# Router queries on fp32 weights as they are, and one first-layer slot in eight multiplied on GpSimd

## Chip, cores and metric

The kernel runs on one core of one Trainium2 chip. The metric is the device time of one execution in microseconds (us), the median of several runs. Beside it one execution was recorded by the hardware profiler; every duration below is from that execution.

## What is computed

An encoder block for 256 tokens (and 16 meta tokens) of width 2048: gated linear attention and differential attention from one input projection, an output projection, and then a retrieval layer (PEER) over 16384 single-neuron experts. The change lies in the last one. Per token and head (8 heads) it makes a query, scores it against two sets of 128 sub-keys, takes the best 16 of each, the best 16 of the 256 sums, and reads those 16 experts' rows `u` and `v` of 2048 numbers:

```python
qb = (xb @ w_q).reshape(TB, PEER_HEADS, 2, PEER_DKEY)
s = jnp.einsum('thpc,hpnc->thpn', qb, sub_keys).astype(jnp.float32)
sv, si = lax.top_k(s, K)
...
cv, ci = lax.top_k(cand, K)
eidx = jnp.take_along_axis(cidx, ci, axis=-1)
g = jax.nn.softmax(cv, axis=-1)
u = u_tab[eidx]
vv = v_tab[eidx]
a = jax.nn.gelu(jnp.einsum('thkd,td->thk', u, xb).astype(jnp.float32), approximate=False)
return jnp.einsum('thk,thkd->td', (g * a).astype(vv.dtype), vv)
```

The dot products of `u` with the token (`thkd,td->thk`) are the first expert layer. A token has 8 x 16 = 128 such **slots**.

## The kernel before

Tokens stand in two tiles of 128 (`tt` = 0, 1), one token per partition. Up to about 1150 us of the profiled execution the kernel does the two attention branches and the output projection. Products with weights go through `proj` (L190): the fp32 weights (`raw`) are split by `load_half` (L163) into a rounded half `hi` (ACT, L185) and a remainder `lo` (a subtraction, L186), and TensorE (PE) makes three products of them, L200 to L202, with the activations split likewise.

The router follows. `hg` (L667, L668) is the normalized input of the layer, transposed and split into two halves. `queries(h)` makes the queries of head `h` with `proj`, where `lo` is computed on DVE for head 0 and on POOL (GpSimd) for the others; then the sub-key scores (L790), and `route(0, h)` (L714), which takes the top 16 (`top16`, L708 to L712) on DVE, with two casts (L721, L732) and one product (L736) on POOL, and leaves the experts' numbers in `ent`. The weights of the queries are loaded by SP's queue.

`gather_dots(tt, h)` (L746) goes over the 16 slots of a head: an indirect DMA issued by POOL (L751) gathers for each of 128 tokens its expert's row of 8 KB, 1 MB in all, and one DVE instruction multiplies it with the tokens `xb` and sums over the 2048 columns (L754):

```python
nc.gpsimd.indirect_dma_start(out=g, out_offset=None, in_=u_tab,
                             in_offset=bass.IndirectOffsetOnAxis(ap=ei[:, k:k + 1], axis=0))
s = h * 16 + k
nc.vector.scalar_tensor_tensor(g, g, 1.0, xb[:, tt, :], op0=ALU.mult, op1=ALU.mult,
                               accum_out=dots[tt][:, s:s + 1])
```

There are 256 such gathers and dots. The gathered tiles alternate between two pools of three buffers, `g` and `gr`; `gr` shares its buffers with the weights `raw`. Between the heads of tile 0 stand the routes of tile 1, between those of tile 1 the steps of `build_w0` on ACT and PE (L815 to L821), which builds the table W0 of the weights of tile 0. Its first use on DVE is at L898. After the last dot (about 1975 us) come W1, the second expert layer, dense on PE for one part of the columns and gathered for the other, and the last norm.

A scheduler writes each engine's queue ahead of time, from the program and its own estimates of durations; on the chip every queue runs in order, and POOL's queue holds its arithmetic and the issue of the gathers alike.

Of the kernel before, what the change touches and what calls it, by code (L numbers as in the profile page):

```python
# [10 lines left out]
F32 = mybir.dt.float32  # L11
F32R = mybir.dt.float32r
# [3 lines left out]
AF = mybir.ActivationFunctionType  # L16
ALU = mybir.AluOpType
# [3 lines left out]
P = 128  # L21
D = 2048
KT = D // P
T = 256
# [16 lines left out]
def block_kernel(ctx: ExitStack, tc: tile.TileContext, A: dict, out: bass.AP):  # L41
    nc = tc.nc

    def pool(name, bufs=1, space=None, side=None, c=ctx):
        kw = {}
        if space is not None:
            kw["space"] = space
        if side is not None:
            kw["side"] = side
        return c.enter_context(tc.tile_pool(name=name, bufs=bufs, **kw))  # L50
# [5 lines left out]
    wp = pool("wp", side="right", c=wpc)  # L56
# [7 lines left out]
    s2p = pool("s2p", c=ph1)  # L64
    ph0 = ExitStack()
    s1p = pool("s1p", c=ph0)

    def pm(shape=(P, N)):
        return pmain.tile(list(shape), F32, tag="pm", name="pm")

    def pa(shape):
        return paux.tile(list(shape), F32, tag="pa", name="pa")
# [57 lines left out]
    for i, (xt, n) in sorted(enumerate(xs), key=lambda e: -(e[0] == 2)):  # L130
# [6 lines left out]
        else:  # L137
# [3 lines left out]
                                           accum_out=s2[:, 1:2])  # L141
# [7 lines left out]
    for k in range(KT):  # L149
        ps = pa([P, N])  # L150
        for i, (xt, n) in enumerate(xs):
            nc.tensor.matmul(ps[:, i * P:i * P + n], lhsT=xt[:, k * P:(k + 1) * P], rhs=sc[i], start=True, stop=True)
        g = vec[:, gm + k:gm + k + 1]
# [6 lines left out]
    def block_of(c0):  # L160
        return (c0 - 32 if c0 > OFF_LR else c0) // 256

    def load_half(w, c0, kh, ncol=256, lo_eng=None, ring=None):  # L163

        src = w[block_of(c0), kh]
        if ring is None:
            parts = [wp.tile([P, 8, ncol], F32, tag="raw", name="raw", bufs=3)]
        elif isinstance(ring, list):
            parts = [s1p.tile([P, 2, ncol], F32, tag=f"s1_{t}", name="raws") for t in ring]
        else:  # L170
            parts = [ring.tile([P, 8, ncol], F32, tag="g", name="rawg")]
        n = 8 // len(parts)
        for i, raw in enumerate(parts):
            nc.sync.dma_start(raw, src[:, i * n:(i + 1) * n, :])
        res = []
        for q in range(2):
            hi = wp.tile([P, 4, ncol], F32R, tag="hi", name="hi", bufs=3)
            lo = wp.tile([P, 4, ncol], F32R, tag="lo", name="lo", bufs=3)
            m = min(n, 4)
            with tc.high_priority():  # L180
                for i in range(4 // m):
                    k0 = 4 * q + i * m
                    raw = parts[k0 // n][:, k0 % n:k0 % n + m, :]
                    ks = slice(i * m, (i + 1) * m)
                    nc.scalar.activation(hi[:, ks], raw, AF.Copy)  # L185
                    (lo_eng or nc.vector).tensor_sub(lo[:, ks], raw, hi[:, ks].bitcast(F32))  # L186
            res.append((hi, lo))
        return res

    def proj(w, c0, act, n, evac, lo_eng=None, ring=None):  # L190

        ps = [pm((P, n)) for _ in range(2)]
        for kh in range(2):
            for q, (hi, lo) in enumerate(load_half(w, c0, kh, lo_eng=lo_eng, ring=ring and ring[kh])):
                for kk in range(4):
                    k = kh * 8 + q * 4 + kk
                    ah, al = act[k][:, 0, :n], act[k][:, 1, :n]
                    for b in range(2):
                        wh, wl = hi[:, kk, b * P:(b + 1) * P], lo[:, kk, b * P:(b + 1) * P]
                        nc.tensor.matmul(ps[b], lhsT=wh, rhs=ah, start=(k == 0), stop=False)  # L200
                        nc.tensor.matmul(ps[b], lhsT=wh, rhs=al, start=False, stop=False)  # L201
                        nc.tensor.matmul(ps[b], lhsT=wl, rhs=ah, start=False, stop=(k == KT - 1))  # L202
        for b in range(2):
            evac(b, ps[b])

    def proj_tokens(w, c0, act, evac):

        ps = [pm((P, 256)) for _ in range(2)]
        for kh in range(2):
            for q, (hi, lo) in enumerate(load_half(w, c0, kh)):  # L210
                for kk in range(4):
                    k = kh * 8 + q * 4 + kk
                    for tt in range(2):
                        ah, al = (act[k][:, i, tt * P:(tt + 1) * P] for i in range(2))
                        nc.tensor.matmul(ps[tt], lhsT=ah, rhs=hi[:, kk], start=(k == 0), stop=False)
                        nc.tensor.matmul(ps[tt], lhsT=ah, rhs=lo[:, kk], start=False, stop=False)
                        nc.tensor.matmul(ps[tt], lhsT=al, rhs=hi[:, kk], start=False, stop=(k == KT - 1))
        for tt in range(2):
            evac(tt, ps[tt])
# [9 lines left out]
    for kh in range(2):  # L229
        raw = bt.tile([P, 8, 32], F32, tag="ow", name="lraw", bufs=4)  # L230
        nc.sync.dma_start(raw, w_lr[kh])
        hi = wp.tile([P, 8, P], F32R, tag="hi", name="lhi", bufs=3)
        lo = wp.tile([P, 8, P], F32R, tag="lo", name="llo", bufs=3)
# [4 lines left out]
        for kk in range(8):  # L238
            k = kh * 8 + kk
# [82 lines left out]
    def gla_head(h):  # L322
# [19 lines left out]
        def ev_r(j):  # L342
# [6 lines left out]
            return f  # L349

        proj(w_in, OFF_GQ + h * 256, hT, T, ev_q)
        proj(w_in, OFF_GK + h * 256, hT, N, ev_k)


# [287 lines left out]
    ring = pool("ring", bufs=3, side="right", c=ringc)  # L642
    hs = s3.tile([P, 2, D], F32, tag="s3", name="hs")
    ssq = cst.tile([P, 2, 8], F32, name="ssq")
    xb = s4.tile([P, 2, D], F32, tag="s4", name="xb")
    hg = [None] * KT
    gf = vrow["g_ffn"]
    w_o = A["c_w_out"]
    for j in range(8):
        xr = bt.tile([P, 2, 256], F32, tag=f"b{j % 2}", name="xr")  # L650
        nc.sync.dma_start(xr, A["x"][0].rearrange("(a p) c -> p a c", p=P)[:, :, j * 256:(j + 1) * 256])

        def ev_o(tt, ps, j=j, xr=xr):
            cs = slice(j * 256, (j + 1) * 256)
            nc.vector.tensor_add(hs[:, tt, cs], ps, xr[:, tt, :])
            jk = bt.tile([P, 256], F32, tag="ow", name="jk", bufs=4)
            nc.scalar.activation(jk, hs[:, tt, cs], AF.Square, accum_out=ssq[:, tt, j:j + 1])

        proj_tokens(w_o, j * 256, yT, ev_o)
        for b in range(2):  # L660
            k = 2 * j + b
            g = vec[:, gf + k:gf + k + 1]
            p2 = pa([P, T])
            for tt in range(2):
                nc.tensor.transpose(p2[:, tt * P:(tt + 1) * P], hs[:, tt, k * P:(k + 1) * P], ident)
            hg[k] = s2p.tile([P, 2, T], F32R, tag=f"s2_{k}", name=f"hg{k}")
            nc.scalar.activation(hg[k][:, 0, :], p2, AF.Copy, scale=g)  # L667
            nc.vector.scalar_tensor_tensor(hg[k][:, 1, :], p2, g, hg[k][:, 0, :].bitcast(F32), op0=ALU.mult,  # L668
                                           op1=ALU.subtract)

    for tt in range(2):
        nc.gpsimd.dma_start(xb[:, tt, :], A["g_ffn"].to_broadcast([P, D]))
# [28 lines left out]
    dots = [gwt[:, tt, 1, :] for tt in range(2)]  # L701
# [44 lines left out]
    def gather_dots(tt, h, ei):  # L746
        for k in range(16):
            i = ngather[0]
            ngather[0] += 1
            g = ring.tile([P, D], F32, tag="g", name="g") if i % 2 else wp.tile([P, D], F32, tag="raw", name="gr", bufs=3)  # L750
            nc.gpsimd.indirect_dma_start(out=g, out_offset=None, in_=u_tab,  # L751
                                         in_offset=bass.IndirectOffsetOnAxis(ap=ei[:, k:k + 1], axis=0))
            s = h * 16 + k
            nc.vector.scalar_tensor_tensor(g, g, 1.0, xb[:, tt, :], op0=ALU.mult, op1=ALU.mult,  # L754
                                           accum_out=dots[tt][:, s:s + 1])

    def weights_of(tt):

# [13 lines left out]

    w_q = A["c_peer_w_q"]

    wait = [(None, ring), (None, ring), (None, [4, 5, 6, 7]), (None, [8, 9, 10, 11]), (None, [12, 13, 14, 15])] + [None] * 3
    eis = {}

    def queries(h):
        qt = bt.tile([P, 2, T], F32, tag=f"b{2 + h % 2}", name="pqt")

        def ev_pq(b, ps):
            with tc.high_priority():
                nc.scalar.activation(qt[:, b, :], ps, AF.Copy)
        proj(w_q, h * 256, hg, T, ev_pq, lo_eng=nc.vector if h == 0 else nc.gpsimd, ring=wait[h])
        s0 = rp.tile([P, 2, P], F32, tag="sS0", name="sS0", bufs=2)
        with tc.high_priority():
            for tt in range(2):
                ps = pa([P, 2, P])
                for p in range(2):
                    nc.tensor.matmul(ps[:, p, :], lhsT=qt[:, p, tt * P:(tt + 1) * P], rhs=skT[h // 2][:, 2 * (h % 2) + p, :],  # L790
                                     start=True, stop=True)
                nc.scalar.activation(s0 if tt == 0 else sS1[:, h], ps, AF.Copy, scale=rst[tt])
            eis[0, h] = route(0, h, s0)
# [259 lines left out]
```

## Time and profile before

| | |
|---|---|
| median of 3 runs | 2615.52 us (2613.9 to 2616.21) |
| profiled execution | 2616.36 us, span of its instructions 2614.6 us |
| mean granted TensorE clock | 0.866 of full speed |
| busy, share of the span | PE 72%, DVE 82%, ACT 42%, POOL 48% |
| indirect gathers on POOL's queue | 348.40 MB, 35.2% of 16 DMA engines |
| transfers of the other large queue | 307.45 MB, 33.8% |

The span runs from the first to the last instruction. Busy time counts arithmetic and the indirect gathers' issue on POOL, no semaphores. "L754" is a line of the kernel; a tile's name stands with the engine and the operation, the output left of the arrow. In brackets stands the idle time of the engine just before an instruction, with what ended it. A view by windows gives busy time per stretch; since the kernel has several stages with different limits, those are read stage by stage.

### The profile page before, as it was taken

Reading aid. Unit: us, or ns where it says so; the run is one execution under the profiler, and the core shown is the slowest. Engines: PE = TensorE matmul, PEld = TensorE weight load, DVE = VectorE, ACT = ScalarE, POOL = GpSimd, SP = SyncE. Lnnn points to the kernel's source line nnn. Section 1 sums busy time; section 2 is a strip of 40 time slices with the busy share of each in tenths; the row PEclk is TensorE's granted clock in tenths of the full one; section 3 lists DMA queues with packets and bytes.
Section 4 is the critical chain, followed back from the end, with each engine's and each line's share of the span. In section 5 each row is a group of like instructions: output and inputs, shape, how many; then the busy total and the mean of one; then the engine's idle time right before and its main releaser. Section 6 shows DMA issues by size and latency. Waiting matters only on the chain. (4 is left out here: it accounts for less than half of the span.)

```text
span 2614.6 us, 37107 instructions
## 1 busy us (share of the span) xinstructions
PE 1889.1 (72%) x13809; PEld 1835.5 (70%) x13809; DVE 2132.0 (82%) x2921; ACT 1106.8 (42%) x2076; POOL 1266.1 (48%) x989
## 2 busy tenths in 40 slices
PE   8999999999999999997500000143006999999997
PEld 7999999999999999997500000132005888999897
DVE  4778877557777775559999999996978899999998
ACT  4565554345655544443200000698006344444444
POOL 1333310000110001028876888885856777777775
PEclk9999999999999999998855555566558999999999
DMA  4445445554444465656699899997993788889886
GB/s 160 146 147 178 146 148 199 187 181 164 165 157 166 167 237 180 227 198 213 227 350 347 322 375 422 421 421 298 418 357 117 263 304 301 315 302 306 302 300 240
DMA packets 110913, 658.38 MB, mean 252 GB/s; under 512 B 14514, under 2 KB 17132, under 8 KB 53116
## 3 DMA queue, kind: packets, MB, share of 16 engines
q0 software_dynamic: 59216, 348.40, 35.2%
q1 hardware_dynamic: 51312, 307.45, 33.8%
q8 instruction: 108, 1.77, 0.3%
q14 instruction: 73, 0.60, 0.1%
q10 hardware_dynamic: 204, 0.17, 0.0%
HBM read 652.78 MB, written 2.10 MB: 250 GB/s over the span
## 5 line engine op out<-in xcount | busy, mean ns | idle before, releaser
L186 DVE TENSOR_TENSOR lo<-raw,hi 128x1024 fp32r<-128x1024 f32 x354 | 453.2, 1281 | 242.7 <-ACT hi L185 240.9
L202 PE MATMUL pm<-hT,lo 128*128 128x256 f32 (+1 forms) x2048 | 577.9, 285 | 7.9 <-DVE lo L186 7.9
L200 PE MATMUL pm<-hT,hi 128*128 128x256 f32 (+1 forms) x2048 | 581.8, 285 | 0.0
L201 PE MATMUL pm<-hT,hi 128*128 128x256 f32 (+1 forms) x2048 | 581.6, 285 | 0.0
L185 ACT ACTIVATE hi<-raw 128x1024 fp32r<-128x1024 f32 x374 | 395.9, 1059 | 363.3 <-PE pm L201 292.5
L202 PEld LDWEIGHTS pm<-hT,lo 128*128 128x128 f32 x2048 | 384.9, 189 | 10.7 <-DVE lo L186 9.0
L200 PEld LDWEIGHTS pm<-hT,hi 128*128 128x128 f32 x2048 | 386.0, 188 | 0.3
L201 PEld LDWEIGHTS pm<-hT,hi 128*128 128x128 f32 x2048 | 386.1, 189 | 0.2
L884 POOL DMA_INDIRECT gv<-in_peer_v_dram,ent x256 | 309.6, 1209 | 140.9 <-DVE hs L887 87.1
L754 DVE SCALAR_TENSOR_TENSOR g<-g,xb 128x2048 f32<-128x2048 f32 x128 | 326.4, 2553 | 15.6 <-DMA g<-in_peer_u_dram,ent 15.3
L768 PE MATMUL pa<-cc,gwt 128*128 128x128 f32 x2 | 0.9, 474 | 462.3 <-DVE gwt L764 462.3
L926 PE MATMUL acc<-vhi,wb 128*128 128x368 f32 x1024 | 334.2, 331 | 0.8 <-DVE wb L898 0.8
L768 PEld LDWEIGHTS pa<-cc,gwt 128*128 128x128 f32 x2 | 0.4, 181 | 462.9 <-DVE gwt L764 462.9
L754 DVE SCALAR_TENSOR_TENSOR gr<-gr,xb 128x2048 f32<-128x2048 f32 x128 | 295.3, 2309 | 28.8 <-DMA gr<-in_peer_u_dram,ent 28.8
L887 DVE SCALAR_TENSOR_TENSOR hs<-gv,gwt,hs 128x576 f32<-128x576 f32 x256 | 280.3, 1095 | 39.3 <-DMA gv<-in_peer_v_dram,ent 35.0
L751 POOL DMA_INDIRECT gr<-in_peer_u_dram,ent x128 | 259.0, 2023 | 78.6 <-DVE gr L754 33.5
L751 POOL DMA_INDIRECT g<-in_peer_u_dram,ent x128 | 250.3, 1956 | 82.4 <-DVE g L754 31.2
L926 PEld LDWEIGHTS acc<-vhi,wb 128*128 128x128 f32 x1024 | 192.4, 189 | 1.0 <-DVE wb L898 1.0
L925 PE MATMUL acc<-vlo,wb 128*128 128x368 f32 x512 | 172.9, 342 | 18.0 <-DVE vlo L917 9.2
L925 PE MATMUL acc<-vlo,wwv 128*128 128x368 f32 x512 | 172.3, 341 | 15.0 <-DVE vlo L917 10.4
L539 POOL DMA_DIRECT2D sw<-dqT x8 | 4.5, 563 | 287.1 <-ACT dqT L552 175.0
L820 PE MATMUL pa<-oh 128*128 128x128 f32 x256 | 58.1, 408 | 104.2 <-ACT oh L819 102.8
(876 smaller groups left out, 4610.6 us busy)
## 6 DMA issues: line engine op xcount, KB each, us to landing
raw<-in_c_w_in_dram SPq DMA_DIRECT2D x128, 1024.0 KB
raw<-in_c_w_branch_gla_dram SPq DMA_DIRECT2D x16, 1024.0 KB
raw<-in_c_w_branch_diff_dram SPq DMA_DIRECT2D x16, 1024.0 KB
raw<-in_c_w_out_dram SPq DMA_DIRECT2D x16, 1024.0 KB
raw<-in_c_peer_w_q_dram SPq DMA_DIRECT2D x11, 1024.0 KB
gv<-in_peer_v_dram,ent POOLq DMA_INDIRECT x256
raws<-in_c_peer_w_q_dram SPq DMA_DIRECT2D x12, 256.0 KB
xt<-in_x_dram SPq DMA_DIRECT2D x2, 1024.0 KB
```

The source lines that it names most:

```text
L185: nc.scalar.activation(hi[:, ks], raw, AF.Copy)
L186: (lo_eng or nc.vector).tensor_sub(lo[:, ks], raw, hi[:, ks].bitcast(F32))
L200: nc.tensor.matmul(ps[b], lhsT=wh, rhs=ah, start=(k == 0), stop=False)
L201: nc.tensor.matmul(ps[b], lhsT=wh, rhs=al, start=False, stop=False)
L202: nc.tensor.matmul(ps[b], lhsT=wl, rhs=ah, start=False, stop=(k == KT - 1))
L751: nc.gpsimd.indirect_dma_start(out=g, out_offset=None, in_=u_tab, in_offset=bass.IndirectOffsetOnAxis(ap=ei[:, k:k + 1], axis=0))
L754: nc.vector.scalar_tensor_tensor(g, g, 1.0, xb[:, tt, :], op0=ALU.mult, op1=ALU.mult, accum_out=dots[tt][:, s:s + 1])
L820: nc.tensor.matmul(ps[:, q, :], lhsT=oh[:, 1, q], rhs=oh[:, 0, q], start=True, stop=True)
L884: nc.gpsimd.indirect_dma_start(out=g, out_offset=None, in_=v_tab, in_offset=bass.IndirectOffsetOnAxis(ap=eis[tt, s // 16][:, s % 16:s % 16 ...
L887: nc.vector.scalar_tensor_tensor(hs[:, tt, DC:], g, gw[tt][:, s:s + 1], hs[:, tt, DC:], op0=ALU.mult, op1=ALU.add)
L925: nc.tensor.matmul(o, lhsT=wh[:, tt, :], rhs=lo[:, ns], start=False, stop=False)
L926: nc.tensor.matmul(o, lhsT=wl[:, tt, :], rhs=hi[:, ns], start=False, stop=last(tt))
```

## The change

The router's queries no longer use halves. `hg` is one fp32 tile instead of two halves, and L668 falls away. `queries` loads the raw weights (`load_raw`) and multiplies them as fp32: for each of 16 row blocks and two column blocks one matmul in place of three, with no `hi` and no `lo`. The halves stay for all other projections.

In `gather_dots` slots 5 and 13 of each head (32 of the 256) are multiplied on POOL (`tensor_mul`, in place, L754 of the new file) and summed by ACT (`activation` with an accumulator, L755). The other 224 dots stay on DVE, as L757. Lines of the router move by one: the gather is L750, the casts L720 and L731, the product L735.

```diff
-            hg[k] = s2p.tile([P, 2, T], F32R, tag=f"s2_{k}", name=f"hg{k}")
-            nc.scalar.activation(hg[k][:, 0, :], p2, AF.Copy, scale=g)
-            nc.vector.scalar_tensor_tensor(hg[k][:, 1, :], p2, g, hg[k][:, 0, :].bitcast(F32), op0=ALU.mult,
-                                           op1=ALU.subtract)
+            hg[k] = s2p.tile([P, T], F32, tag=f"s2_{k}", name=f"hg{k}")
+            nc.scalar.activation(hg[k], p2, AF.Copy, scale=g)
...
             s = h * 16 + k
-            nc.vector.scalar_tensor_tensor(g, g, 1.0, xb[:, tt, :], op0=ALU.mult, op1=ALU.mult,
-                                           accum_out=dots[tt][:, s:s + 1])
+            if s % 8 == 5:
+                nc.gpsimd.tensor_mul(g, g, xb[:, tt, :])
+                nc.scalar.activation(g, g, AF.Copy, accum_out=dots[tt][:, s:s + 1])
+            else:
+                nc.vector.scalar_tensor_tensor(g, g, 1.0, xb[:, tt, :], op0=ALU.mult, op1=ALU.mult,
+                                               accum_out=dots[tt][:, s:s + 1])
...
-        proj(w_q, h * 256, hg, T, ev_pq, lo_eng=nc.vector if h == 0 else nc.gpsimd, ring=wait[h])
+        ps = [pm((P, T)) for _ in range(2)]
+        for kh in range(2):
+            for k0, raw in load_raw(w_q, h * 256, kh, wait[h][kh]):
+                for kk in range(raw.shape[1]):
+                    k = k0 + kk
+                    for b in range(2):
+                        nc.tensor.matmul(ps[b], lhsT=raw[:, kk, b * P:(b + 1) * P], rhs=hg[k], start=(k == 0), stop=(k == KT - 1))
+        for b in range(2):
+            ev_pq(b, ps[b])
```

`load_raw` holds the loads that stood in `load_half`, on the same queue and into the same buffers:

```diff
+    def load_raw(w, c0, kh, where=None):
 
         src = w[block_of(c0), kh]
...
         for i, raw in enumerate(parts):
             nc.sync.dma_start(raw, src[:, i * n:(i + 1) * n, :])
+        return [(8 * kh + i * n, raw) for i, raw in enumerate(parts)]
```

**The order on POOL.** The scheduler's queue of POOL from the first route on (`sif`, `hlf`, `ohx` belong to a route, `g` is a gathered tile). Before:

```order
L186 TENSOR_TENSOR lo<-raw,hi 128x1024
L721 CAST sif<-si 128x32
L186 TENSOR_TENSOR lo<-raw,hi 128x1024
L732 CAST hlf<-hl 128x32
L186 TENSOR_TENSOR lo<-raws,hi 128x512 x2
L736 TENSOR_TENSOR ohx<-ohx,sif 128x512
L186 TENSOR_TENSOR lo<-raws,hi 128x512 x2
L751 DMA g<-in_peer_u_dram,ent 128x2048 x3
L186 TENSOR_TENSOR lo<-raw,hi 128x1024
```

And now:

```order
L720 CAST sif<-si 128x32
L731 CAST hlf<-hl 128x32
L735 TENSOR_TENSOR ohx<-ohx,sif 128x512
L750 DMA g<-in_peer_u_dram,ent 128x2048 x5
L754 TENSOR_TENSOR g<-g,xb 128x2048
L720 CAST sif<-si 128x32
L750 DMA g<-in_peer_u_dram,ent 128x2048
L731 CAST hlf<-hl 128x32
L750 DMA g<-in_peer_u_dram,ent 128x2048
L735 TENSOR_TENSOR ohx<-ohx,sif 128x512
L750 DMA g<-in_peer_u_dram,ent 128x2048 x2
L754 TENSOR_TENSOR g<-g,xb 128x2048
```

The subtractions between a route's operations are gone, and products stand between the gathers; the first multiplies the third of the five tiles gathered ahead of it.

Further on, with the buffers' numbers, POOL's queue among the slots of tile 1 before:

```order
L751 DMA gr_15537<-in_peer_u_dram,ent_13686 128x2048
L751 DMA g_15714<-in_peer_u_dram,ent_13686 128x2048
L751 DMA gr_15543<-in_peer_u_dram,ent_13686 128x2048
L751 DMA gr_15549<-in_peer_u_dram,ent_13686 128x2048
L751 DMA g_15720<-in_peer_u_dram,ent_13686 128x2048
```

And now:

```order
L750 DMA g_15201<-in_peer_u_dram,ent_13670 128x2048
L750 DMA gr_14999<-in_peer_u_dram,ent_13670 128x2048
L750 DMA g_15208<-in_peer_u_dram,ent_13670 128x2048
L750 DMA gr_15005<-in_peer_u_dram,ent_13670 128x2048
L750 DMA g_15294<-in_peer_u_dram,ent_13670 128x2048
L750 DMA gr_15012<-in_peer_u_dram,ent_13670 128x2048
L754 TENSOR_TENSOR g_15201<-g_15201,xb_12563 128x2048
L750 DMA gr_15057<-in_peer_u_dram,ent_13670 128x2048
```

Where only gathers stood, a product stands behind the fifth gather after its own tile's. Of the 32 products five stand two gathers behind their own, eight four, and nineteen five. Counted by the gathers ahead of each, six fall among the slots that were worked on before 1300 us, eight among those up to 1540 us, and eighteen after.

## Rows read from the trace of the kernel before

**Rows 1.** The page: busy us (share of the span) x instructions

```profile
PE 1889.1 (72%) x13809; PEld 1835.5 (70%) x13809; DVE 2132.0 (82%) x2921; ACT 1106.8 (42%) x2076; POOL 1266.1 (48%) x989
```

**Rows 2.** Windows: us, engines' busy us (instructions), granted clock, DMA share, GB/s

```profile
1185.00:1300.00 115.00, 79.17 (x563) 75.49 (x561) 111.27 (x196) 30.13 (x56) 96.90 (x61) 0.87 0.62 218
1300.00:1540.00 240.00, 0.66 (x2) 0.29 (x2) 235.91 (x446) 5.65 (x22) 189.21 (x109) 0.50 0.91 342
1540.00:1655.00 115.00, 0.00 (x0) 0.00 (x0) 107.62 (x96) 0.00 (x0) 100.68 (x48) 0.50 1.01 418
1655.00:1822.00 167.00, 58.77 (x259) 52.78 (x259) 133.63 (x117) 162.03 (x451) 127.72 (x60) 0.61 0.94 391
1822.00:1950.00 128.00, 0.00 (x0) 0.00 (x0) 114.13 (x101) 0.76 (x2) 95.60 (x46) 0.51 0.92 368
1950.00:2615.00 665.00, 586.55 (x3329) 552.90 (x3329) 604.81 (x823) 302.47 (x506) 471.37 (x444) 0.96 0.81 276
```

**Rows 3.** Lines by form, DVE, 1180 to 1300: operation, count, busy us, mean ns, idle

```profile
L754 DVE SCALAR_TENSOR_TENSOR g<-g,xb 128x2048 f32<-128x2048 f32 x16 | 66.1, 4134 | 2.8 <-DMA g<-in_peer_u_dram,ent 2.8
...
L754 DVE SCALAR_TENSOR_TENSOR gr<-gr,xb 128x2048 f32<-128x2048 f32 x1 | 2.3, 2291 | 0.0
```

**Rows 4.** The same view, DVE, 1185 to 1540

```profile
L734 DVE TENSOR_TENSOR ohx<-hlf,cc 128x512 f32<-128x512 f32 x15 | 14.0, 930 | 1.2 <-POOL hlf L732 0.9
```

**Rows 5.** The same view, DVE, 1540 to 1980

```profile
L754 DVE SCALAR_TENSOR_TENSOR gr<-gr,xb 128x2048 f32<-128x2048 f32 x89 | 203.7, 2292 | 28.8 <-DMA gr<-in_peer_u_dram,ent 28.8
L754 DVE SCALAR_TENSOR_TENSOR g<-g,xb 128x2048 f32<-128x2048 f32 x74 | 169.3, 2292 | 12.8 <-DMA g<-in_peer_u_dram,ent 12.5
```

**Rows 6.** Timeline of DVE: start, length us, instruction, idle before

```profile
1191.02 7.71 DVE L754 SCALAR_TENSOR_TENSOR g<-g,xb 128x2048 f32<-128x2048 f32 x1 [2.80 <-DMA g<-in_peer_u_dram,ent]
...
1204.81 0.67 DVE L734 TENSOR_TENSOR ohx<-hlf,cc 128x512 f32<-128x512 f32 x1
...
1205.68 2.27 DVE L754 SCALAR_TENSOR_TENSOR g<-g,xb 128x2048 f32<-128x2048 f32 x1
```

**Rows 7.** Timeline of POOL, same columns

```profile
1185.21 1.31 POOL L751 DMA_INDIRECT g<-in_peer_u_dram,ent  x1 [0.17 <-issue]
1186.82 0.96 POOL L751 DMA_INDIRECT g<-in_peer_u_dram,ent  x1 [0.30 <-issue]
...
1189.06 2.38 POOL L186 TENSOR_TENSOR lo<-raw,hi 128x1024 fp32r<-128x1024 f32 x1
...
1191.54 2.39 POOL L186 TENSOR_TENSOR lo<-raw,hi 128x1024 fp32r<-128x1024 f32 x1
...
1194.03 2.55 POOL L186 TENSOR_TENSOR lo<-raws,hi 128x512 fp32r<-128x512 f32 x2
```

**Rows 8.** Timeline in the third stretch

```profile
1600.10 2.29 DVE L754 SCALAR_TENSOR_TENSOR g<-g,xb 128x2048 f32<-128x2048 f32 x1 [0.19 <-DMA g<-in_peer_u_dram,ent]
1601.02 2.18 POOL L751 DMA_INDIRECT g<-in_peer_u_dram,ent  x1 [0.30 <-issue]
...
1602.59 2.29 DVE L754 SCALAR_TENSOR_TENSOR gr<-gr,xb 128x2048 f32<-128x2048 f32 x1 [0.19 <-DMA gr<-in_peer_u_dram,ent]
```

**Rows 9.** Windows, 1100 to 1200: columns as in rows 2

```profile
1100.00:1200.00 100.00, 98.60 (x832) 98.02 (x831) 61.47 (x115) 48.96 (x87) 36.19 (x26) 1.00 0.57 203
```

**Rows 10.** Timeline of PE at the first route's keys

```profile
1179.13 0.60 PE L790 MATMUL pa<-skT,pqt 128*128 128x128 f32 x4
1179.49 0.36 PE L200 MATMUL pm<-hg,hi 128*128 128x256 f32 x1
```

**Rows 11.** Windows of the tile lo: PE, PEld, DVE, POOL busy us

```profile
1170.70:1185.20 14.50, 10.33 (x38) 6.97 (x38) 0.00 (x0) 10.25 (x6) 1.00 0.20 73
```

**Rows 12.** Lines by form, ACT, 0 to 60

```profile
L136 ACT ACTIVATE sqx<-xt 128x2048 f32<-128x2048 f32 x1 | 1.9, 1909 | 2.4 <-DMA xt<-in_x_dram 2.4
...
L136 ACT ACTIVATION_READ_ACCUMULATOR sqx<-xt 128x1 f32 x1 | 0.2, 187 | 0.0
```

**Rows 13.** Timeline of DVE at the end of the W0 build

```profile
1822.37 0.42 DVE L898 TENSOR_TENSOR wb<-W,wb 128x256 fp32r<-128x256 f32 x1 [21.72 <-ACT wb L897]
```

More of the change, by code (lines that the diff above doesn't have):

```diff
@@ L161, in block_of @@
         return (c0 - 32 if c0 > OFF_LR else c0) // 256
-    def load_half(w, c0, kh, ncol=256, lo_eng=None, ring=None):
+    def load_raw(w, c0, kh, where=None):
         src = w[block_of(c0), kh]
[L166 to L169, printed above, removed]
+        if where is None:
+            parts = [wp.tile([P, 8, 256], F32, tag="raw", name="raw", bufs=3)]
+        elif isinstance(where, list):
+            parts = [s1p.tile([P, 2, 256], F32, tag=f"s1_{t}", name="raws") for t in where]
         else:
-            parts = [ring.tile([P, 8, ncol], F32, tag="g", name="rawg")]
+            parts = [where.tile([P, 8, 256], F32, tag="g", name="rawg")]
         n = 8 // len(parts)
@@ L174, in load_half @@
             nc.sync.dma_start(raw, src[:, i * n:(i + 1) * n, :])
+        return [(8 * kh + i * n, raw) for i, raw in enumerate(parts)]
+    def load_half(w, c0, kh, ncol=256):
+        (_, raw), = load_raw(w, c0, kh)
         res = []
@@ L178, in load_half, with proj @@
             lo = wp.tile([P, 4, ncol], F32R, tag="lo", name="lo", bufs=3)
-            m = min(n, 4)
             with tc.high_priority():
[L181 to L186, printed above, removed]
+                src = raw[:, 4 * q:4 * q + 4, :]
+                nc.scalar.activation(hi, src, AF.Copy)
+                nc.vector.tensor_sub(lo, src, hi.bitcast(F32))
             res.append((hi, lo))
         return res
-    def proj(w, c0, act, n, evac, lo_eng=None, ring=None):
+    def proj(w, c0, act, n, evac):
         ps = [pm((P, n)) for _ in range(2)]
         for kh in range(2):
-            for q, (hi, lo) in enumerate(load_half(w, c0, kh, lo_eng=lo_eng, ring=ring and ring[kh])):
+            for q, (hi, lo) in enumerate(load_half(w, c0, kh)):
                 for kk in range(4):
@@ L773, in block_kernel @@
     w_q = A["c_peer_w_q"]
-    wait = [(None, ring), (None, ring), (None, [4, 5, 6, 7]), (None, [8, 9, 10, 11]), (None, [12, 13, 14, 15])] + [None] * 3
+    wait = [(None, ring), (None, ring), (None, [4, 5, 6, 7]), (None, [8, 9, 10, 11]), (None, [12, 13, 14, 15])] + [(None, None)] * 3
     eis = {}
```

## The prediction

> **What bounds the kernel now.** I read the busy shares first, then busy time by stretch, then the first-layer dots grouped by form, then engines against the clock inside one stretch. DVE is the busiest engine over the span [rows 1], but that is a mean over stages. The stretches [rows 2] tell them apart. In 1185 to 1300 DVE is busy 111.27 of 115 us, in 1300 to 1540 235.91 of 240: DVE is the bound. From 1540 to 1655 the DMA share is 1.01: there the transfers are the bound. From 1655 to 1822 ACT works 162.03 of 167 us on W0. From 1950 on PE has 586.55 of 665, and nothing of the change reaches there. So I treat three stretches apart: 1 (to 1300), 2 (to 1540), 3 (to the last dot, about 1975).
>
> A dot costs 2.29 us wherever it is alone [rows 5]. In stretch 1 the `g` dots take 4134 ns [rows 3], and the timeline shows why: the dot at 1191.02 takes 7.71 us [rows 6] while POOL runs `lo` subtractions at 1191.54 and 1194.03 [rows 7]; these take 2.39 and 2 x 1.28 us, no longer than the 2.38 of 1189.06 with no dot beside it, and the dot ends 2.1 us after the last of them. With POOL silent the dot at 1205.68 takes 2.27. A DVE product and a POOL product exclude each other: whichever is later waits for the whole of the other. That is the row on which this prediction turns.
>
> Steady gathering has a rhythm [rows 8]: a gather issued at 1601.02 is held until the dot of 1600.10 is over (about 1602.31) and ends 0.9 us later, which is what a free issue lasts (0.96 at 1186.82, [rows 7]); 0.30 us on, POOL starts the next. One gather per dot, one dot every 2.49 us: POOL has no gap of its own for more.
>
> **The change part by part.** The sum is made against the profiled execution, 2616.36 us; the median is 2615.52, 0.8 less, so both serve.
>
> *Queries without halves.* It removes per head 4 ACT casts and 4 subtractions on POOL in stretch 1 (DVE for head 0), and 16 DVE subtractions for `hg`. The ACT casts lie beside a PE that is busy 98.60 of 100 us [rows 9]; the DVE ones beside the same PE; I cost both at nothing. The weight loads on SP's queue stay as they are, and their tiles come free after the matmuls instead of after the subtractions: nothing. PE: 96 single products of 0.1185 us (98.60 / 832, [rows 9]), 11.4 us a head, become 32 fp32 ones. The two fp32 128-column products at 1179.13 have let the next one in after 0.36 us [rows 10], so 0.18 each, 0.36 for 256 columns: 11.5 us a head. At the other end, with the 0.60 that the pair lasts, 0.60 each and 19 us. The near row is the spacing, so PE gains and loses nothing; at 19 us head 0 would be 8 us late and the later heads lie beside DVE work. The POOL part is worth most. Seventeen dots took 68.4 us in stretch 1 [rows 3], and would take 17 x 2.29 = 38.9: -29.5. The compare of 128x512 stretched in the same way, 930 ns [rows 4] against 0.67 free [rows 6], 15 times: -3.9. Together **-33.4**. Before its first gather POOL spent 10.25 of 14.5 us on `lo` [rows 11], and the route's casts stood behind them; I take **-8** and keep 0 and -10 as ends.
>
> *Products of 32 slots on GpSimd.* Their price: a POOL product of two operands takes 1.28 us for 128x512 and 2.39 for 128x1024 [rows 7], so 1.11 per 512 more, 4.6 us for 128x2048. The Trainium skill, GPSIMD Engine Reference, section 3.1, has 4497 ns for this size; by it the sum would be some 4 us less.
>
> The order gives six products to stretch 1, eight to stretch 2, eighteen to stretch 3. In stretches 1 and 2 DVE is the bound, and loses 4.6 us to each product where it saves a dot of 2.3: 6 x 2.3 = **+13.8** and 8 x 2.3 = **+18.4**. In stretch 1 the product stands only 2 to 4 gathers behind its own, so POOL waits for the tile itself, which holds the next gathers: 5 x 2 = **+10** (ends 0 and +20).
>
> In stretch 3 the sum per eight slots is 8 x 2.49 = 19.92 before. Lower end: only the exclusion counts, 7 x 2.29 + 4.62 = 20.65, +0.73 per product, +13 in all. Upper end: the product comes on top, and the gather behind it waits for one more whole dot, 4.6 + 2.3 = 6.9, +124. I take 4.6 each: for that time POOL issues nothing and DVE multiplies nothing, the eighth gather still needs a gap of its own behind a dot or the product, and the slot's buffer comes back late, after product and ACT sum (1.91 us for 2048 columns, [rows 12], and its read) instead of after 2.29. With six buffers and a gather held until a dot ends, POOL cannot make it up: 18 x 4.6 = **+82.8**.
>
> *Cover.* Now DVE stands 21.72 us for W0 [rows 13]. With 7 products among those dots they last about 32 us longer, while ACT gets 7 sums of 2.1: some **-15** comes back. The ACT sums elsewhere fall where ACT works 5.65 of 240 us [rows 2]: nothing. The last stage keeps its order: 0, give or take 5.
>
> Sum: -33.4 - 8 + 13.8 + 10 + 18.4 + 82.8 - 15 = **+68.6**: 2685 us, 2.6% slower. Its own range, with part of the way to the ends above, is 2645 to 2715.
>
> **The rivals.**
>
> A. *Transfers stay the bound in stretch 3* (price 0.73 per product). For it: the DMA share is 1.01, with several tiles in flight, so a POOL that stops for 4.6 us may not be missed. Against: every gather is held to a dot's end [rows 8]. Then it is +13 in place of +82.8 and only -5 of the W0 wait comes back: +9, about **2625**, and it can land on either side of no change. The Trainium skill, SBUF — State Buffer, section "A bandwidth-pool intuition that's wrong (but worth ruling out)", says that HBM is almost always the end-to-end bottleneck; by that this rival would win. The trace agrees for that stretch alone, with 418 GB/s; in stretches 1 and 2 the transfers run at 218 and 342 GB/s while DVE is full [rows 2].
>
> B. *Faster: the products run beside the dots.* If a POOL product with an output over its own input does not lock DVE out, each saves DVE its whole dot of 2.29 and adds nothing: stretch 1 gives -33.4 - 8 + 10 - 6 x 2.29 = -45, stretch 2 -18, stretch 3, held by transfers, nothing: about **2553**. It decides if dots beside L754 products last 2.3 us. Against it stand the dots of 7.71 and 4134 ns [rows 3, 6]: same operation, same engine.
>
> C. *POOL stands still for more than the product*: it waits for its own tile, or behind a sum that stands in ACT's row between W0 steps, and gathers dry up. At 6.9 per product stretch 3 has 41 us more, and with +20 in stretch 1 another 10: **2726 to 2736**.
>
> **How the numbers follow.** Forecast 0.70, A 0.14, B 0.06, C 0.10. The range takes the forecast's own 2645 to 2715, the upper part of A and the lower part of C: 2622 to 2728, which leaves out B, a quarter of A, most of C and the edges of the forecast, 0.2 in all. No change means within 0.2%, about 5 us, which is what a measurement of this kernel can tell. Faster: B and a quarter of A, 0.10. Same: 0.05, from A. Slower: 0.85.
>
> **What would show it.** Right: 32 POOL products near 4.6 us alone, up to 6.9 where a dot was first; DVE dots in stretch 1 at 2.3 us but for those beside a product; in stretch 3 a DMA share that falls from 1.01 to about 0.85, with DVE waiting for tiles; the first gather some 8 us earlier after the first route; the L898 wait gone or small. Wrong: a DMA share that stays near 1 (A), dots of 2.3 us beside products (B), POOL's waits for tiles or for ACT above 2 us each (C), or a query stage in which PE takes 19 us a head and the first route starts late.

## The result, and the profile after

The changed kernel takes 2653.52 us (median, 2652.69 to 2658.48), against 2614.79 for the kernel before in the same session: a ratio of 1.0152, with a 95% interval of 1.0134 to 1.0169. It is slower by 38.7 us where 68.6 were forecast; the time lies inside the forecast's range. The profiled execution has a span of 2652.3 us against 2614.6, 37.7 more.

Where the time went is counted best by slots, since both kernels gather the same 256 tiles. The rows of dots (and, after, of ACT sums) give the time at which so many slots were done; by the 94th the routes lie behind or nearly so in both.

| us | before | after | difference |
|---|---|---|---|
| 17th slot done | 1299.3 | 1266.1 | -33.2 |
| 94th | 1540.3 | 1545.6 | +5.3 |
| 192nd | 1783.2 | 1834.6 | +51.4 |
| 256th (last) | 1975.1 | 2020.7 | +45.6 |
| end of the span | 2614.6 | 2652.3 | +37.7 |

Busy time by stretch after, cut at 17, 94, 137, 193 and 256 slots done (the cuts of [rows 2] lie at 17, 94, 141, 199 and 249; columns as there):

```profile
1182.00:1266.00 84.00, 74.92 (x350) 65.33 (x349) 67.69 (x147) 16.61 (x36) 51.72 (x35) 0.96 0.74 290
1266.00:1546.00 280.00, 22.02 (x100) 18.52 (x98) 263.12 (x484) 27.09 (x50) 214.18 (x123) 0.54 0.81 296
1546.00:1670.00 124.00, 0.00 (x0) 0.00 (x0) 107.94 (x77) 10.02 (x10) 100.15 (x49) 0.50 0.91 362
1670.00:1835.00 165.00, 46.91 (x201) 41.09 (x201) 141.86 (x100) 146.45 (x384) 135.18 (x64) 0.57 0.92 363
1835.00:2021.00 186.00, 13.42 (x58) 12.16 (x58) 153.57 (x115) 43.16 (x97) 137.87 (x66) 0.52 0.88 343
2021.00:2652.00 631.00, 588.01 (x3329) 556.55 (x3329) 575.95 (x809) 303.50 (x506) 456.37 (x438) 0.97 0.82 280
```

The stretch that ran at a DMA share of 1.01 and 418 GB/s [rows 2] now runs at 0.91 and 362: the transfers are no longer full. DVE is not full there either, 107.94 of 124 us. Neither is the bound alone; they wait for each other.

The dots by form, in the first stretch (1180 to 1266) and in the third (1546 to 2021), with the first use of W0, and POOL's products over the span:

```profile
L757 DVE SCALAR_TENSOR_TENSOR g<-g,xb 128x2048 f32<-128x2048 f32 x13 | 31.6, 2433 | 9.7 <-DMA g<-in_peer_u_dram,ent 9.7
L722 DVE TENSOR_TENSOR cand<-sv 128x256 f32<-128x256 f32 x4 | 11.3, 2814 | 0.0
```

```profile
L757 DVE SCALAR_TENSOR_TENSOR gr<-gr,xb 128x2048 f32<-128x2048 f32 x90 | 272.1, 3036 | 64.2 <-DMA gr<-in_peer_u_dram,ent 64.1
L757 DVE SCALAR_TENSOR_TENSOR g<-g,xb 128x2048 f32<-128x2048 f32 x54 | 136.2, 2522 | 5.3 <-DMA g<-in_peer_u_dram,ent 5.3
L909 DVE TENSOR_TENSOR wb<-W,wb 128x256 fp32r<-128x256 f32 x1 | 0.4, 426 | 1.4 <-ACT wb L908 1.4
```

```profile
L754 POOL TENSOR_TENSOR g<-g,xb 128x2048 f32<-128x2048 f32 x32 | 155.6, 4863 | 2.9 <-DMA g<-in_peer_u_dram,ent 2.2
```

In the first stretch the dots fell from 4134 ns [rows 3] to 2433. In the third they rose from 2292 [rows 5] to 3036 and 2522. The 21.72 us at W0's first use [rows 13] are now 1.4. A product takes 4863 ns in the mean, its own wait for a dot included.

One cycle of the third stretch, from the timeline of DVE, POOL and ACT:

```profile
1602.48 0.94 POOL L750 DMA_INDIRECT gr<-in_peer_u_dram,ent  x1 [0.30 <-issue]
1603.72 0.94 POOL L750 DMA_INDIRECT g<-in_peer_u_dram,ent  x1 [0.30 <-issue]
1604.67 4.51 POOL L754 TENSOR_TENSOR g<-g,xb 128x2048 f32<-128x2048 f32 x1
1604.85 6.49 DVE L757 SCALAR_TENSOR_TENSOR gr<-gr,xb 128x2048 f32<-128x2048 f32 x1 [3.48 <-DMA gr<-in_peer_u_dram,ent]
1609.21 1.91 ACT L755 ACTIVATE g<-g 128x2048 f32<-128x2048 f32 x1 [21.25 <-POOL g L754]
...
1611.27 2.28 DVE L757 SCALAR_TENSOR_TENSOR gr<-gr,xb 128x2048 f32<-128x2048 f32 x1
1611.62 2.79 POOL L750 DMA_INDIRECT gr<-in_peer_u_dram,ent  x1 [2.44 <-DVE gr L757]
...
1613.48 2.28 DVE L757 SCALAR_TENSOR_TENSOR g<-g,xb 128x2048 f32<-128x2048 f32 x1
```

The product starts at 1604.67 and lasts 4.51. The dot of 1604.85 lasts 6.49, 2.28 and the rest of the product. From 1604.66, when the last gather was out, no gather starts until 1611.62, and that one ends only behind the dot of 1611.27. Six dots then start one after another every 2.21 us on tiles that have piled up, and the missing gathers come back as a hole: DVE waited 3.48 us for a tile at 1604.85, and a wait like it, of 2.6 to 3.8 us, stands in every cycle of eight slots.

### The profile page after: what moved, and what is told of

Same layout as the page of the kernel before. It is cut to its first block, busy times and chain, and to the rows that moved or that the text cites. A ratio compares the mean times of both kernels' runs of the same rounds, so it can differ in the third digit from the quotient of the medians.

```text
span 2652.3 us, 36471 instructions
## 1 busy us (share of the span) xinstructions
PE 1907.2 (72%) x13553; PEld 1842.6 (69%) x13553; DVE 2118.2 (80%) x2837; ACT 1138.6 (43%) x2102; POOL 1259.3 (47%) x987
## 3 DMA queue, kind: packets, MB, share of 16 engines
q0 software_dynamic: 59216, 348.40, 35.1%
## 5 line engine op out<-in xcount | busy, mean ns | idle before, releaser
L186 ACT ACTIVATE hi<-raw 128x1024 fp32r<-128x1024 f32 x352 | 372.8, 1059 | 336.9 <-PE pm L202 275.8
L757 DVE SCALAR_TENSOR_TENSOR gr<-gr,xb 128x2048 f32<-128x2048 f32 x128 | 381.5, 2991 | 68.2 <-DMA gr<-in_peer_u_dram,ent 68.0
L895 POOL DMA_INDIRECT gv<-in_peer_v_dram,ent x256 | 303.4, 1185 | 138.3 <-DVE hs L898 89.3
L898 DVE SCALAR_TENSOR_TENSOR hs<-gv,gwt,hs 128x576 f32<-128x576 f32 x256 | 277.8, 1085 | 45.6 <-DMA gv<-in_peer_v_dram,ent 41.1
L750 POOL DMA_INDIRECT gr<-in_peer_u_dram,ent x128 | 233.7, 1826 | 111.1 <-DVE gr L757 77.0
L757 DVE SCALAR_TENSOR_TENSOR g<-g,xb 128x2048 f32<-128x2048 f32 x96 | 236.5, 2464 | 16.6 <-DMA g<-in_peer_u_dram,ent 16.6
L750 POOL DMA_INDIRECT g<-in_peer_u_dram,ent x128 | 201.1, 1571 | 76.4 <-issue 30.6
L755 ACT ACTIVATE g<-g 128x2048 f32<-128x2048 f32 x32 | 61.4, 1918 | 355.3 <-POOL g L754 355.3
L754 POOL TENSOR_TENSOR g<-g,xb 128x2048 f32<-128x2048 f32 x32 | 155.6, 4863 | 2.9 <-DMA g<-in_peer_u_dram,ent 2.2
```

The costliest lines, as they stand in the source:

```text
L186: nc.scalar.activation(hi, src, AF.Copy)
L754: nc.gpsimd.tensor_mul(g, g, xb[:, tt, :])
L895: nc.gpsimd.indirect_dma_start(out=g, out_offset=None, in_=v_tab, in_offset=bass.IndirectOffsetOnAxis(ap=eis[tt, s // 16][:, s % 16:s % 16 ...
L898: nc.vector.scalar_tensor_tensor(hs[:, tt, DC:], g, gw[tt][:, s:s + 1], hs[:, tt, DC:], op0=ALU.mult, op1=ALU.add)
```

## Experiments

Ratios are against the kernel before on the same chip, with 95% intervals.

### The two halves apart

The queries alone (all dots on DVE):

```diff
-            if s % 8 == 5:
-                nc.gpsimd.tensor_mul(g, g, xb[:, tt, :])
-                nc.scalar.activation(g, g, AF.Copy, accum_out=dots[tt][:, s:s + 1])
-            else:
-                nc.vector.scalar_tensor_tensor(g, g, 1.0, xb[:, tt, :], op0=ALU.mult, op1=ALU.mult,
-                                               accum_out=dots[tt][:, s:s + 1])
+            nc.vector.scalar_tensor_tensor(g, g, 1.0, xb[:, tt, :], op0=ALU.mult, op1=ALU.mult,
+                                           accum_out=dots[tt][:, s:s + 1])
```

> The change's queries alone; all 256 dots stay on DVE. Theory T (the products cost more than their own place, the queries give back a part): the subtractions no longer stretch the first dots and the first route is shorter, the seventeenth dot ends some 40 us earlier, the rest is as before: 2575 us (2565 to 2585). Rival Q (the queries give nothing that lasts, because transfers bound the rest): 2605 to 2615, and the products alone then cost some 40 us.

Measured: 2587.87 us, 0.9912 (0.9893 to 0.9930). The products alone, on the queries of before (the same hunk, applied to the old file):

> The change's 32 products alone, on the queries of before with their subtractions on POOL. T: 2615 plus what the change lies above the queries alone, about 78 us: 2693 us (2680 to 2710). Q: about 2655 us.

Measured: 2695.73 us, 1.0323 (1.0305 to 1.0340). T holds for the products alone; for the queries alone it named 2575 (at most 2585) and got 2588. The seventeenth slot is done 39.2 us earlier, as T said, but the lead is 29.8 us at the 94th slot (1510.5), 28.2 at the 192nd and 20.6 at the last (1954.5). Rival Q falls: transfers set the pace from the 94th slot to the 192nd, and the lead held there. It shrank in the last 64 slots, and the rows show one place for it. In the queries alone the scheduler's queue leaves 22 tiles of `gr` for the end, where the kernel before leaves 16 (POOL's queue in the trace), and with three buffers in place of six a slot takes 3.5 us there instead of 2.5. DVE's dots in the queries alone, 1880 to 1954, and the busy times of the same window:

```profile
L753 DVE SCALAR_TENSOR_TENSOR gr<-gr,xb 128x2048 f32<-128x2048 f32 x22 | 50.4, 2292 | 26.2 <-DMA gr<-in_peer_u_dram,ent 26.2
```

```profile
1880.00:1954.00 74.00, 0.00 (x0) 0.00 (x0) 47.98 (x43) 0.00 (x0) 29.45 (x19) 0.50 0.79 292
```

So the queries are worth some 23 us (2613.06 x 0.0088) and the products cost 63 on them (1.0152 - 0.9912 = 0.0240 of 2614), 84 on the old queries (0.0323). The last stage differs too: from the last slot to the end 639.5 us before, 632.1 here, 631.6 in the changed kernel, 640.5 with the products alone. What makes these 8 us was not tried.

### The product taken out, its sum left

```diff
-                nc.gpsimd.tensor_mul(g, g, xb[:, tt, :])
                 nc.scalar.activation(g, g, AF.Copy, accum_out=dots[tt][:, s:s + 1])
```

> The change without the product on POOL: the 32 tiles go to ACT's sum as they were gathered, so these 32 slots lack the product with the token. T (the exclusion of DVE and POOL is the cost): about 10 dots fewer where DVE is the bound, and the transfers' pace of 2.49 us a slot after that: 2550 us (2535 to 2565). Rival R (the cost is the buffers' late return after a sum on ACT and the slot's place in the queues): 2600 us or above.

Measured: 2565.86 us, 0.9834 (0.9818 to 0.9851). T misses its range (2535 to 2565) by 0.9 us, and rival R falls: without the POOL product the 88 us above it (2653.52 - 2565.86) are gone, though tiles still come back late behind a sum. R has a small place. POOL's own waits between 1490 and 1745 in this run:

```profile
POOL g L750 <- ACT g L754: 27.1, 10, 7.8
POOL gr L750 <- DVE gr L756: 14.8, 7, 3.2
```

Ten gathers wait 27.1 us for buffers behind sums on ACT. From the 94th to the 192nd slot this run needs 258.9 us (1486.5 to 1745.4), the queries alone 244.6, the changed kernel 289.0: of the 44 us between the last two, 14 come with the late sums and 30 with the product itself.

### The same products without the exclusion

The price was read from an exclusion of DVE and POOL where both read two operands from SBUF, the memory in which the gathered tiles and the tokens stand. The products stay; DVE's dots read the tokens elsewhere, from PSUM, where the outputs of this kernel's matmuls stand (the lines that open and close the PSUM pools are left out here):

```diff
+    def load_xp(tt):
+        xp_[tt] = pxb.tile([P, D], F32, tag="xp", name="xp")
+        for n in range(4):
+            nc.scalar.activation(xp_[tt][:, n * 512:(n + 1) * 512], xb[:, tt, n * 512:(n + 1) * 512], AF.Copy)
...
-                nc.vector.scalar_tensor_tensor(g, g, 1.0, xb[:, tt, :], op0=ALU.mult, op1=ALU.mult,
+                nc.vector.scalar_tensor_tensor(g, g, 1.0, xp_[tt], op0=ALU.mult, op1=ALU.mult,
                                                accum_out=dots[tt][:, s:s + 1])
```

> The change, with the tokens copied into PSUM by ACT, one tile of tokens at a time, and DVE's 224 dots reading them there; the 32 products on POOL still read them in SBUF. The queries' PSUM tiles go from 4 and 4 to 2 and 2. T (a DVE dot with both operands in SBUF and a POOL product exclude each other): the dots beside a product last 2.3 us, and a gather need not wait for a dot's end; 2500 to 2560 us, 2540 the likeliest, if DVE reads PSUM as fast. Rival R (late buffers and places in the queues): 2630 us or above. Rival S (the two engines exclude each other wherever the operands lie): 2650 us, dots of 6 us beside products. The Trainium skill, SBUF — State Buffer, says that a DVE instruction with two SBUF inputs contends with a GpSimd instruction that reads SBUF; by that T would hold.

Measured: 2604.70 us, 0.9968 (0.9957 to 0.9978), 49 us below the changed kernel. Rivals R and S fall. The time is not T's, but the rows are. By form, 1180 to 1980, and one product with a dot in it:

```profile
L757 DVE SCALAR_TENSOR_TENSOR gr<-gr,xp 128x2048 f32<-128x2048 f32 x128 | 292.1, 2284 | 43.7 <-DMA gr<-in_peer_u_dram,ent 38.9 <-ACT xp L868 4.9
L757 DVE SCALAR_TENSOR_TENSOR g<-g,xp 128x2048 f32<-128x2048 f32 x96 | 219.4, 2286 | 71.6 <-DMA g<-in_peer_u_dram,ent 71.3
```

```profile
L754 POOL TENSOR_TENSOR g<-g,xb 128x2048 f32<-128x2048 f32 x32 | 144.9, 4528 | 9.3 <-DMA g<-in_peer_u_dram,ent 8.7
L750 POOL DMA_INDIRECT gr<-in_peer_u_dram,ent x128 | 122.2, 955 | 110.8 <-DVE gr L757 65.6 <-issue 18.9 <-DVE tk L709 6.8
```

```profile
1695.99 4.54 POOL L754 TENSOR_TENSOR g<-g,xb 128x2048 f32<-128x2048 f32 x1
1699.49 2.29 DVE L757 SCALAR_TENSOR_TENSOR gr<-gr,xp 128x2048 f32<-128x2048 f32 x1 [2.79 <-DMA gr<-in_peer_u_dram,ent]
...
1712.51 0.94 POOL L750 DMA_INDIRECT g<-in_peer_u_dram,ent  x1 [7.04 <-ACT g L755]
```

All 224 dots take 2.28 us in the mean, the one of 1699.49 too, which begins inside a product. The products take 4528 ns, no more than alone. Late buffers remain: the gather of 1712.51 had stood 7.04 us for a sum on ACT. Even the issue of a `gr` gather has become shorter: 955 ns against 1826 in the changed kernel and 2023 before. What T missed is the start: the seventeenth slot is done at 1311.7, 45.6 us later than in the changed kernel, because here the scheduler put six routes ahead of the first dot. The other 239 slots take 646.5 us against 754.6.

The next three leave the queries their PSUM and use only the four banks that are free when the queries are done, so that heads 0 and 1 of tile 0 stay in SBUF. Their first lines, in this order:

```diff
-            if s % 8 == 5:
+            xt_ = xp_[tt] if (tt == 0 and h >= 2) else xb[:, tt, :]
+            if tt == 0 and h >= 2 and s % 8 == 5:
```

```diff
-            if s % 8 == 5:
+            xt_ = xp_[tt] if (tt == 1 or h >= 2) else xb[:, tt, :]
+            if (tt == 1 or h >= 2) and s % 8 == 5:
```

```diff
-            if s % 8 == 5:
+            xt_ = xp_[tt] if (tt == 1 or h >= 2) else xb[:, tt, :]
+            if False:
```

> The change's queries; products only for the slots of heads 2 to 7 of tile 0 (12 of them), and there DVE's dots read the tokens in PSUM, in the four banks that the queries leave; the rest of the dots as before, on DVE from SBUF. T (exclusion of two-operand SBUF reads is the price of a product): from the queries alone, 2588 us, each product takes one dot of 2.3 us off a full DVE: 2560 us (2550 to 2575). Rival R (the places in the queues and the late buffers are the price): 2590 to 2620.

> As the run before, with PSUM tokens and products for all slots but those of heads 0 and 1 of tile 0 (28 products). T: the first stretch of the queries alone (seventeenth dot near 1260 us) and the pace of the run with all tokens in PSUM behind it (646 us for the other 239): 1906 us to the last dot and 2540 in all (2530 to 2560). Rival R: 2590 or above.

> As the run before without any product: all dots on DVE, from PSUM but for heads 0 and 1 of tile 0. T: gathers are no longer held to a dot's end (0.95 us each), which is worth nothing where DVE is full or the transfers are the bound: 2585 us (2575 to 2592), the queries alone. Rival H (the held gathers cost time by themselves): 2565 or below.

Measured: 12 products 2575.64 us, 0.9854 (0.9830 to 0.9877); 28 products 2576.11, 0.9856 (0.9833 to 0.9879); none 2573.68, 0.9849 (0.9826 to 0.9871). The three are not told apart. With the exclusion gone 28 products cost 2 us, where 32 cost 66 with it (2653.52 - 2587.87): the exclusion is shown to be most of the price. But the products bring nothing either, and there T was wrong, for 28 products by 36 us. And the run without products is 14 us faster than the queries alone, past the range of T and short of H's.

The 2 us are a balance, not a price of nothing. DVE's wait for W0 with 28 products and with none, and the issue of `g` gathers with 28:

```profile
DVE wb L924 <- ACT wb L923: 6.1, 1, 6.1
```

```profile
DVE wb L924 <- ACT wb L923: 22.0, 1, 22.0
```

```profile
L750 POOL DMA_INDIRECT g<-in_peer_u_dram,ent x109 | 102.8, 943 | 164.0 <-DVE g L758 86.5 <-ACT g L756 36.1 <-issue 25.6
```

From the 94th to the 192nd slot, W0's wait left out, 28 products need 261.4 us and none 240.5: 21 us more for the twelve products there, 1.7 each. ACT builds W0 in that stretch and the sums come late (a product that ends at 1632.45 is summed from 1637.30 on), so that six gathers stand 36.1 us for buffers behind them. This is rival R's price; a wait for W0 that is 16 us shorter hides it, together with a lead of 6 us at the 94th slot. With W0's wait put back, the 32 products cost 85 us with the exclusion (65.7 and 19.7 of the wait), the 28 without it 18 (2.4 and 15.9).

The issue of `gr` gathers by form in the queries alone (1260 to 1955) and in the run with PSUM tokens and no products (1268 to 1931):

```profile
L750 POOL DMA_INDIRECT gr<-in_peer_u_dram,ent x128 | 242.6, 1895 | 96.8 <-DVE gr L753 49.7 <-issue 28.2 <-DVE sv L710 6.7
```

```profile
L750 POOL DMA_INDIRECT gr<-in_peer_u_dram,ent x128 | 123.8, 967 | 209.7 <-DVE gr L758 145.4 <-DVE tk L709 12.2 <-DVE sv L710 11.3
```

A gather was not only waiting for its buffer behind a dot, it was held by the dot; freed, it is issued in 0.97 us. But the 14 us do not show that the held gathers cost time. At the 94th slot the two runs are level (1511.3 and 1510.5), and nearly all of the lead at the last slot (1930.2 and 1954.5) comes in slots 224 to 256: 80.5 us against 101.7. There the queries alone work off their 22 tiles of `gr` on three buffers, while in all runs with PSUM tokens `g` and `gr` are mixed to the end, at 2.5 us a slot. That is the scheduler's order, which changed along with the operand. The 12 products brought nothing because the last slot was bound elsewhere: at the 94th slot they are 6 us ahead of none (1505.1 and 1511.3), and at the last one they are level (1929.4 and 1930.2), with DVE standing 22.8 and 22.0 us for W0 in between.

### The third stretch's price, and the wait for W0

```diff
-            if s % 8 == 5:
+            if tt == 1 and s % 8 == 5:
```

> The change with its products for tile 1 alone (16), all tokens in SBUF. The forecast's price of the third stretch (4.6 us each, 15 back from W0's wait): 2588 + 59 = 2647 us. T with the price read from the changed kernel (52 us more over the last 162 slots with 21 products, so 2.5 each, and 21 back from W0's wait): 2588 + 40 - 21 = 2607 us (2600 to 2620).

Measured: 2619.65 us, 1.0014 (1.0001 to 1.0026), so 32 us over the queries alone. That is little more than half of the forecast's 59 for these slots. The price read from the changed kernel (2.5 gross) was 13 us too low in the sum; it counted 21 products in that stretch, where the trace has 18, which would make it 2.9. The other 16 products make the remaining 34 us (2653.52 - 2619.65). A product costs 2.0 us in tile 1, net of 20 us that the wait for W0 gave back (0.7 here), and 2.1 in tile 0.

Last, W0's first use bound to a late slot (an ACT write of one column, ahead of the conversion that DVE waits for), on the runs with PSUM tokens and no or 12 products:

```diff
                 src = Ws[tt][:, 2 * g:2 * g + 2, :]
+                if tts == (0,):
+                    nc.scalar.activation(wh[:, 0, tt, 0:1], dots[1][:, HD:HD + 1], AF.Copy)
```

> The run without products and with tokens in PSUM, where besides the first use of W0 is bound to a late slot of tile 1, so that DVE does not stand for it with dots queued behind. T (gathers and transfers set the third stretch once DVE and POOL no longer exclude each other, and the wait of 22 us for W0 is time lost from them): 2554 us (2546 to 2564). Rival W (the wait only moves behind the last dot): 2570 or above.

> The same late first use of W0, with the 12 products of heads 2 to 7 of tile 0 on POOL and their dots from PSUM. T: the 6 us that the products were ahead at the 94th slot are no longer eaten by the wait for W0: 2549 us (2540 to 2562), up to 6 under the run without products. Rival W: 2570 or above.

Measured: without products 2554.50 us, 0.9772 (0.9754 to 0.9790); with 12 products 2556.80, 0.9787 (0.9767 to 0.9807). Rival W falls. The third stretch of the first of them, in windows and in DVE's waits (1510 to 1920):

```profile
1510.00:1905.00 395.00, 59.32 (x259) 53.32 (x259) 364.38 (x329) 163.90 (x454) 147.85 (x158) 0.55 1.01 417
```

```profile
DVE g L758 <- DMA g<-in_peer_u_dram,ent: 13.3, 60, 1.1
DVE gr L758 <- DMA gr<-in_peer_u_dram,ent: 12.0, 58, 0.9
...
DVE wb L926 <- ACT wb L925: 0.4, 1, 0.4
```

The DMA share is 1.01 for 395 us: this stretch is now held by the transfers from end to end, and while they are full a product taken off DVE does not shorten it. So the second run, with 12, is not faster, against T's 2549: its lead of 2.6 us at the 94th slot is gone at the last. The two are the fastest kernels of this study and not told apart; the first is 2.3% under the one before and 3.7% under the changed one (2554.50 / 2653.52). The same late W0 with all 28 products, where the late sums would no longer be hidden, was not run.

## Why the prediction was right, point by point

**The mechanism, right.** The exclusion that [rows 6, 7] showed for subtractions holds for the products: dots of 6.49 us beside products of 4.51, 2.28 once DVE reads one operand from PSUM. The Trainium skill, SBUF — State Buffer, section "SBUF: two separate sides", calls this an exclusive lock on a port that DVE needs with two SBUF inputs and GpSimd needs to read; the pair of 6.49 and 2.28 us agrees with it.

**The price of a product, right.** 4.6 us by extrapolation, 4.50 to 4.56 in 24 of the 32; the other eight, with a dot ahead, took 5.7 to 6.0. The 4497 ns of the Trainium skill, GPSIMD Engine Reference, section 3.1, are nearer still.

**The queries, -41.4 forecast.** By the seventeenth dot it is more or less that (-39.2 in the run with the queries alone); in the end 23. The step that failed is that a lead in the first stretch would last: 9 us went by the 94th slot and 9 more behind it, nearly all in the last 64 slots, where the longer run of `gr` tiles stands. The first 9 were largely work put off: between the two slots DVE is busy 248.6 of 250 us (236.9 of 241 before) and runs 22 `MAX8` of `sv` from `tk`, a step of the routes, against 18. Of the 8 us for the first route, 4.4 came (10.1 us from its start to the first gather, 14.5 before), and 1.8 of them went because the route started later, behind longer queries on PE. PE's rows by form, 1150 to 1300, 64 of them to a head (the mean is a pipelined length, not a spacing):

```profile
L793 PE MATMUL pm<-hg,raw 128*128 128x256 f32 x352 | 81.0, 388 | 0.0
L793 PE MATMUL pm<-hg,rawg 128*128 128x256 f32 x64 | 14.3, 379 | 0.0
```

An fp32 product is two of these records, and 20 of them took 4.32 us from one start to the next: 0.43 us for 256 columns, 13.8 a head, where 0.36 and 11.5 were taken from a 128-column pair. The first gather came at 1182.65, 2.6 us earlier.

**First and second stretch, +42.2 for 14 products.** Between the changed kernel and the queries alone there are 35.1 us at the 94th slot (1545.6 and 1510.5). Right in size, in part by luck, for the single terms are not. The first stretch was forecast at +23.8 and cost 6.0 (1266.1 and 1260.1): four products fell into the first 17 slots, not six, and POOL waited 2.2 us for its own tiles where 10 were taken. The second was forecast at +18.4 and cost 29.1: it had ten products, not eight, at 2.9 each and not 2.3, since routes were stretched as well. `cand` took 2814 ns against 0.4 free, and a 16-column operation of the route stands at 1319 ns between 1266 and 1546.

**Third stretch, +82.8: the term that failed.** From the 94th slot to the last the changed kernel needs 475.1 us against 434.8 before, +40.3, and with the 20 us of W0's wait put back it is 60: 3.4 us for each of 18 products where 4.6 were taken. In the steady part, slots 94 to 192, it is 289.0 against 242.9, so 3.8 for each of twelve. In the last 64 slots only 14 us remain beside W0's gain, 2.4 for each of six; there the changed kernel also leaves fewer tiles of `gr` for the end (12, before 16). What the step overlooked is the pile: during a product transfers under way still land, so most often four or five dots behind it start 2.21 us after the one before instead of 2.49, which makes up 1.1 to 1.4 us of the product. The lower end, 0.73, was too low for the reason that the forecast gave: no gather goes out while the product and the dot behind it last, and the hole returns as a wait of 2.6 to 3.8 us for a tile. The steady price lies in the middle between the two ends. The forecast's reason also named the slot's buffer that comes back late; in the changed kernel POOL did not wait for a sum on ACT, and the runs without the exclusion show that price.

**Cover, -15 forecast.** The wait for W0 fell from 21.7 to 1.4, -20. Right in kind.

**The last stage, 0.** It gave 7.9 us back. Not foreseen, and open.

Together, of the 31 us that the forecast of the span was too high, 27.5 come from the third stretch with its cover, 7.9 from the last stage, and 4.5 go the other way in the first two.

**The rivals.** A would have had a DMA share near 1; it is 0.91. B needed dots of 2.3 us beside products; with SBUF tokens they are 6.5. C needed long waits of POOL for tiles or for ACT: it waited 2.2 us in all for its tiles, as the products' row above shows, and not for ACT's sums. All three were partly right about another kernel: with the tokens in PSUM the products do run beside the dots (B), the transfers are the bound wherever gathers go out in time (A), and gathers stand behind sums between W0's steps on ACT (C).

## What to carry to other kernels

Work moved to GpSimd is not taken off DVE while both read two operands from SBUF: here a product of 4.5 us held DVE's dots of 2.3 us and the gathers behind it, so that the pair did one thing at a time. Look for a long DVE row that begins just after a POOL row and ends a dot's length after it; putting DVE's second operand into PSUM took the exclusion away here (6.49 us and 2.28). And before offloading, ask what bounds the stretch once the offloaded part is free: here it was the transfers, so the gain left was to remove what stood in their way. The wait for W0 was worth 19 us in the runs without products; late sums on ACT and a queue that left the last tiles to half of the buffers stood there too, and were not taken out by themselves. Compare the queues of two kernels before a difference is put down to the operand that was changed.

## What the runs showed that was not expected

An indirect gather issued by POOL is held by a two-operand DVE dot in the same way: 1.9 to 2.0 us each with the tokens in SBUF, 0.95 to 0.97 with them in PSUM. Whether that alone is worth time was not shown. Without any product the run with PSUM tokens is 14 us faster (2587.87 and 2573.68), but it differs in the order of the last tiles too, and in the dots' mean, which went from 2.34 to 2.29 us as routes' products on POOL no longer held them. Where transfers set the pace, a slot takes 2.49 us with held and with freed gathers alike.

A very small DVE operation with one input waits for a POOL product even when the dots do not. In the run with 28 products and PSUM tokens:

```profile
1404.75 4.51 POOL L755 TENSOR_TENSOR g<-g,xb 128x2048 f32<-128x2048 f32 x1
...
1406.26 3.05 DVE L728 TENSOR_SCALAR hl<-ci 128x16 uint32<-128x16 uint32 x1
```

It takes 0.17 us when free and ends here with the product, at 1409.3; the dot before it, from PSUM, began at 1403.45 and was not touched. Which property of the operation does it was not tried.
